# The expert loop of a hybrid block: TensorE, ScalarE and VectorE in an order set by hand

## Chip, cores and metric

One core of a Trainium2 chip runs the whole program. The metric is the device time of one execution in microseconds, the median of several runs.

## What is computed

The program is one layer of a hybrid model over 2048 tokens of width 1024: a token mixer with four branches, then a mixture of experts, then a norm. The change lies in the experts alone. A router gives each token two of 32 experts (`NE`), and

```python
def expert_block(args):
    xb, e = args
    return (jax.nn.silu(xb @ w1[e]) * (xb @ w3[e])) @ w2[e]
...
y_assign = out[dest].astype(jnp.float32) * weights[order][:, None]
return jax.ops.segment_sum(y_assign, tok_sorted, num_segments=n_tok).astype(h.dtype)
```

with `w1` and `w3` of 1024 x 512 and `w2` of 512 x 1024 in float32: 6.3 MB of weights for each expert, and 128 tokens on average.

## The kernel before

The functions of the experts stand inside `ffn`. The first 128 tokens of an expert are computed with float32 numbers split into a high part and the remainder: `split` (line 1224 casts on ScalarE, line 1225 subtracts on VectorE), and `mm3` (lines 1368 to 1370) makes three matmuls of each product. A panel is 128 x 1024 numbers, 0.52 MB. An expert has twelve: four of `w1`, four of `w3`, four of `w2`. `unit` (line 808) loads one into a buffer `mraw` and splits it into `mhi` and `mlo`. There are 16 raw buffers and 12 pairs of parts (`RAW, PARTS = 16, 12`), so a panel of the next expert takes the pair that the same panel of this expert leaves.

Tokens 129 to 192 of an expert are its small blocks, of 32 tokens each. They use the raw panels: `up_rest` and `down_rest` call `quarters` (line 930), which puts four column groups side by side, inside `tc.If` on the count of tokens (`guard`, loaded at line 1006 into a register of TensorE and of GpSimd). Their sums stand in two banks of PSUM of their own, `hu` and `hd` ("hf0" and "hf1"); two banks "tr" hold transposes, two "mm" the sums of `up`, two "sc" those of `down`.

The loop over the experts runs one expert ahead in parts. Its body, for expert e, is: the small up block (`up_rest`), its activation and gate (`gate_rest`), the first layer (`up`, with activation at line 903 and gate at 904), the transposes of the small result (`plain`, "hq"), the transposes of the next expert's gathered rows (`turn`, line 869 and 870, and `turn_rest`, line 877, with copies of the token weights at lines 884 and 892), the gather of the rows after those (`fetch`, on GpSimd), the panels of the next first layer, then the second layer of the expert before (`down`), this expert's `w2` panels, the small down block and the transposes of h (`parts`). Results are added to the rows in memory by indirect DMAs on GpSimd (line 908). `beyond` makes a table for tokens above 192 and is called in the fifth expert.

A transpose takes its bank, and the copy out of it follows at once in the program's text:

```python
def turned_into(put, src, r, n, w=128):
    for c in range(0, n, 512 // r):
        ...
        pt = psum("tr")
```

The text is not the order in which an engine runs: a scheduler lays out each engine's list before the run from its own estimates, and keeps only the dependencies. A `tc.If` stays a unit. On the chip each engine then works its list from the front.

Of the kernel before, what the change touches and what calls it, by code (L numbers as in the profile page):

```python
# [570 lines left out]
def ffn(tc, G, A, out, bcast, rsqrt, split, mm3, MT, MR, X1, FR, mid):  # L571
# [236 lines left out]
    def unit(src, q=nc.sync, eng=nc.vector):  # L808

        raw = rp.tile([128, 1024], F32, name="mraw")  # L810
        q.dma_start(raw, src)
        hi, lo = (wr.tile([128, 1024], F32R, name=n, bufs=PARTS) for n in ("mhi", "mlo"))
        split(raw, hi, lo, eng)
        return hi, lo, raw

# [39 lines left out]
    def turned_into(put, src, r, n, w=128):  # L855

        for c in range(0, n, 512 // r):
            m = min(n - c, 512 // r)
            pt = psum("tr")
            for k in range(m):  # L860
                nc.tensor.transpose(pt[:, k * r:(k + 1) * r], src[:, (c + k) * 128:(c + k + 1) * 128], G.ident[:r, :r])
            put(slice(c, c + m), pt[:, :m * r].rearrange("p (k t) -> p k t", t=r))

    def parts(src, n, name):

        hi, lo = (wp.tile([128, n, 128], F32R, name=name + c) for c in "hl")

        def put(c, v):
            nc.scalar.copy(hi[:, c], v)
            nc.vector.tensor_sub(lo[:, c], v, hi[:, c].bitcast(F32))  # L870
        turned_into(put, src, 128, n)
        return hi, lo

    def plain(src, n, name):

        t = wp.tile([128, n, 64], F32, name=name)
        turned_into(lambda c, v: nc.scalar.copy(t[:, c], v), src, 64, n)
        return t

    def turn(xg):  # L880

        p = parts(xg, 8, "x")
        w = wp.tile([128, 1], F32, name="w0", bufs=2)
        nc.scalar.copy(w, xg[:, D:D + 1])
        return p, w

    def turn_rest(xg):

        p = plain(xg, 8, "xq")
# [3 lines left out]
        return p, w  # L893

    def up(xw, w1, w3):

        x, w = xw
        pa = [psum("mm"), psum("mm")]
        for p, ws in zip(pa, (w1, w3)):
            mm3(p, lambda k: (x[0][:, k], x[1][:, k]),  # L900
                lambda k: tuple(t[:, (k % 2) * 512:(k % 2) * 512 + 512] for t in ws[k // 2][:2]), range(8))
        h = wp.tile([128, FF], F32, name="mh0")
        nc.scalar.activation(h, pa[0], AF.Silu)
        nc.vector.scalar_tensor_tensor(h, pa[1], w, h, op0=OP.mult, op1=OP.mult)
        return h
# [8 lines left out]
    def down(h, w2, dst, rest=()):  # L914

        y = wp.tile([128, D], F32, name="my0")
        py = [psum("sc"), psum("sc")]
        for c, (p, ws) in enumerate(zip(py, w2)):
            o = slice(512 * c, 512 * c + 512)
            mm3(p, lambda k: (h[0][:, k], h[1][:, k]), lambda k: tuple(t[:, o] for t in ws[k][:2]), range(4))  # L920
            nc.vector.tensor_mul(y[:, o], p, m5[:, o])  # L921
# [14 lines left out]
    def up_rest(xw, w1, w3, guard):  # L936

        w = [w1, w3]
        quarters(hu, 8, guard, lambda k, j: xw[0][:, k, j * 32:j * 32 + 32],
                 lambda k, g: w[g // 2][k // 2][2][:, (k % 2) * 512 + (g % 2) * 256:][:, 0:256])  # L940

    def gate_rest(xw):
        h = wp.tile([64, FF], F32, name="mh1")
        nc.scalar.activation(h, hu[0:64], AF.Silu)
        for j in range(2):
            o = slice(j * 256, j * 256 + 256)
            nc.vector.scalar_tensor_tensor(h[:, o], h[:, o], xw[1][:, j:j + 1], hu[64:128, o], op0=OP.mult, op1=OP.mult)
        return h

    def down_rest(h, w2, guard, e_):  # L950

        quarters(hd, 4, guard, lambda k, j: h[:, j * 2 + k % 2, (k // 2) * 32:(k // 2) * 32 + 32],
                 lambda k, g: w2[k][2][:, g * 256:g * 256 + 256])
# [12 lines left out]
    def in_weights(e_, q=nc.sync, eng=lambda n, u: nc.vector):  # L966
        f2 = lambda n, u: A[n][e_][:, 2 * u:2 * u + 2].rearrange("p k n -> p (k n)")
        return [[unit(f2(n, u), q, eng(n, u)) for u in range(4)] for n in ("e1", "e3")]
# [41 lines left out]
    x = turn(rows_[0]), turn_rest(rows_[1])  # L1010
# [4 lines left out]
    with tc.issue_after(listed.ins):  # L1015
        w13 = in_weights(0, eng=lambda n, u: nc.gpsimd if n == "e1" and u < 2 else nc.vector)
    last = None
    for e_ in range(NE + 1):
        if e_ < NE:
# [4 lines left out]
            up_rest(x[1], *w13, guard)  # L1024
            h1 = gate_rest(x[1])
            h = up(x[0], *w13)
            t1 = plain(h1, 4, "hq")
            q = nc.sync if e_ else nc.gpsimd
            if e_ + 1 < NE:
                x = turn(rows_[0]), turn_rest(rows_[1])  # L1030
# [21 lines left out]
    with tc.For_i(0, nov, 1) as it:  # L1052
# [23 lines left out]
        h = up(turn(gather(ix, 0, nullcontext)), w1, w3)  # L1076
        down(parts(h, 4, "h"), w2, ixs)
# [514 lines left out]
```

## Time and profile before

| | |
|---|---|
| median of 3 runs | 3157.36 us (3155.1 to 3159.68) |
| profiled execution | 3149.57 us, span 3147.7 us |
| TensorE busy | 2852.9 us, 91% |
| VectorE busy | 1827.1 us, 58% |
| ScalarE busy | 1160.4 us, 37% |
| the loop over the experts | 2238.7 to 3094.1 us of the span |

Busy time is the union of an engine's instructions; the ends of matmuls are modelled, so a row of matmuls that overlap counts as busy while the next one starts every 0.23 us. An engine's wait is the gap before an instruction, and what ended it is named behind the arrow. PEld is TensorE's weight loading; a "q" behind an engine's name is its sequencer, which evaluates branches and loads registers.

### The profile page before, as it was taken

The numbers are of one execution on the slowest core, as the hardware profiler recorded it, in microseconds if no ns is written. First come the engines' busy times: TensorE is split into PE (matmuls) and PEld (weight loads), VectorE is DVE, ScalarE is ACT, GpSimd is POOL, SyncE is SP. The second block draws the span as 40 slices with busy tenths as digits, with TensorE's granted clock in tenths as the row PEclk, the third lists the DMA queues.
The fourth block names the chain that finished last, engine by engine and source line by source line (L and its number), as shares of the span: only waits on it lengthen the run. The fifth ranks groups of instructions, "written<-read, shape, count | busy, mean of one in ns | idle before, by whom it ended". The sixth has DMA issues, their size and how long they took to land. (4 is left out here: it accounts for less than half of the span.)

```text
span 3147.7 us, 43618 instructions
## 1 busy us (share of the span) xinstructions
PE 2852.9 (91%) x15893; PEld 2229.4 (71%) x15893; DVE 1827.1 (58%) x2870; ACT 1160.4 (37%) x1722; POOL 583.6 (19%) x522
## 2 busy tenths in 40 slices
PE   7998999999867999899999999999588998999992
PEld 3887887777655677677777777888466676666662
DVE  4624125978776587433334334566678677777674
ACT  5411122322345032232223212322466566666552
POOL 3300010000014021013334333000211212112211
PEclk8999999999978899999999999999798999999996
DMA  7636244423128376765436434554788788888876
GB/s 295 243 111 210 87 158 154 144 81 110 52 72 277 124 225 202 254 237 194 134 120 207 131 125 149 187 169 148 268 292 276 262 300 279 303 289 286 273 235 238
DMA packets 245984, 621.48 MB, mean 197 GB/s; under 512 B 31128, under 2 KB 81464, under 8 KB 242008
## 3 DMA queue, kind: packets, MB, share of 16 engines
q1 hardware_dynamic: 211312, 506.17, 46.6%
q0 software_dynamic: 34416, 111.88, 12.4%
q8 instruction: 163, 2.67, 0.3%
q14 instruction: 93, 0.76, 0.1%
HBM read 484.86 MB, written 137.28 MB: 198 GB/s over the span
## 5 line engine op out<-in xcount | busy, mean ns | idle before, releaser
L1225 DVE TENSOR_TENSOR mlo<-mraw,mhi 128x1024 fp32r<-128x1024 f32 x382 | 447.8, 1225 | 61.4 <-ACT mhi L1224 61.3
L1224 ACT CAST mhi<-mraw 128x1024 fp32r<-128x1024 f32 x384 | 382.5, 1046 | 53.9 <-PE ps_mm L1370 16.1
L1368 PE MATMUL ps_mm<-hb1h,wlo 128*128 128x512 f32 x800 | 319.9, 400 | 2.6 <-DVE wlo L1225 2.6
L1369 PE MATMUL ps_mm<-hb1l,whi 128*128 128x512 f32 x800 | 317.9, 397 | 0.0
L1370 PE MATMUL ps_mm<-hb1h,whi 128*128 128x512 f32 x800 | 317.8, 397 | 0.0
L1519 ACT ACTIVATE ev<-ps_mm 128x512 f32<-128x512 f32 x128 | 76.3, 598 | 612.1 <-PE ps_mm L1370 511.5
L1225 DVE TENSOR_TENSOR wlo<-wraw,whi 128x1024 fp32r<-128x1024 f32 x164 | 214.9, 1319 | 145.1 <-ACT whi L1224 145.0
L1368 PE MATMUL ps_mm<-hb0h,wlo 128*128 128x512 f32 x672 | 270.0, 402 | 16.0 <-DVE wlo L1225 12.5
L1369 PE MATMUL ps_mm<-hb0l,whi 128*128 128x512 f32 x672 | 269.7, 401 | 0.0
L1370 PE MATMUL ps_mm<-hb0h,whi 128*128 128x512 f32 x672 | 267.9, 399 | 0.0
L1224 ACT CAST whi<-wraw 128x1024 fp32r<-128x1024 f32 x176 | 182.1, 1045 | 169.2 <-PE ps_mm L1370 69.8
L1569 POOL TENSOR_TENSOR macc<-macc,ev 128x512 f32<-128x512 f32 x96 | 165.8, 1727 | 309.0 <-DVE ev L1568 306.2
L1568 DVE TENSOR_TENSOR ev<-ev,ps_tr 128x512 f32<-128x512 f32 x96 | 65.8, 687 | 249.9 <-PE ps_tr L1370 243.4
L1369 PE MATMUL ps_mm<-mlo,xh 128*128 128x512 f32 x512 | 203.7, 398 | 6.9 <-PEq L928 3.0
L1368 PE MATMUL ps_mm<-mhi,xl 128*128 128x512 f32 x512 | 206.2, 403 | 1.8 <-ACT mhi L1224 1.4
L1370 PE MATMUL ps_mm<-mhi,xh 128*128 128x512 f32 x512 | 202.9, 396 | 2.5 <-PEq L928 2.2
L908 POOL DMA_INDIRECT d_X<-my,sct x51 | 100.7, 1974 | 444.6 <-DVE my L921 289.6
L1368 PEld LDWEIGHTS ps_mm<-hb1h,wlo 128*128 128x128 f32 x800 | 151.3, 189 | 37.0 <-issue 3.4
L1370 PEld LDWEIGHTS ps_mm<-hb1h,whi 128*128 128x128 f32 x800 | 151.2, 189 | 33.0 <-issue 2.4
L1369 PEld LDWEIGHTS ps_mm<-hb1l,whi 128*128 128x128 f32 x800 | 151.3, 189 | 32.2 <-issue 1.9
L1368 PEld LDWEIGHTS ps_mm<-hb0h,wlo 128*128 128x128 f32 x672 | 128.0, 191 | 45.9 <-DVE wlo L1225 14.3
L1369 PEld LDWEIGHTS ps_mm<-hb0l,whi 128*128 128x128 f32 x672 | 128.1, 191 | 29.3 <-issue 3.2
(588 smaller groups left out, 5898.7 us busy)
## 6 DMA issues: line engine op xcount, KB each, us to landing
mraw<-e SPq DMA_DIRECT2D x372, 512.0 KB
wraw<-wg SPq DMA_DIRECT2D x80, 512.0 KB
wraw<-wt SPq DMA_DIRECT2D x40, 512.0 KB
aw<-adaw SPq DMA_DIRECT2D x64, 256.0 KB
d_GS<-ev SPq DMA_DIRECT2D x64, 256.0 KB
ev<-d_GS POOLq DMA_DIRECT2D x64, 256.0 KB, 4.4
wraw<-wg POOLq DMA_DIRECT2D x24, 512.0 KB, 4.3
d_FR<-hb0h SPq DMA_DIRECT2D x22, 512.0 KB
```

The costliest lines, as they stand in the source:

```text
L908: d = nc.gpsimd.indirect_dma_start(out=out, out_offset=bass.IndirectOffsetOnAxis(ap=dst, axis=0), in_=y, in_offset=None, compute_op=OP.add)
L1224: nc.scalar.copy(hi, raw)
L1225: eng.tensor_sub(lo, raw, hi.bitcast(F32))
L1368: nc.tensor.matmul(ps, wl, xh, start=start and n == 0, stop=False)
L1369: nc.tensor.matmul(ps, wh, xl, start=False, stop=False)
L1370: nc.tensor.matmul(ps, wh, xh, start=False, stop=stop and n == len(ks) - 1)
L1519: nc.scalar.activation(g, ps, AF.Sigmoid)
L1568: nc.vector.tensor_mul(g, g, ps)
L1569: nc.gpsimd.tensor_add(acc, acc, g)
```

## The change

Each helper is cut into what TensorE does and what ScalarE and VectorE do with the result, so that the loop can place the halves apart. `in_order`, called between the pieces, chains all instructions of TensorE, ScalarE and VectorE traced since its last call, each behind the one before it on its engine (edges without a semaphore). SyncE and GpSimd stay with the scheduler.

```diff
+    def in_order():
+        traced = nc.cur_bb.bb.instructions
+        if queues.get("block") is not traced:
+            queues.clear()
+            queues.update(block=traced, at=len(traced))
+        for i in traced[queues["at"]:]:
+            if i.engine in (mybir.EngineType.PE, mybir.EngineType.Activation, mybir.EngineType.DVE):
+                if i.engine in queues:
+                    tc.add_manual_dep(i, queues[i.engine].name, mybir.DependencyInfo(
+                        mybir.DependencyClass.NoSync, mybir.DependencyReason.DATA), reason="in order")
+                queues[i.engine] = i
+        queues["at"] = len(traced)
...
-            pt = psum("tr")
+            pt = psum("tr") if bank is None else bank
...
     for e_ in range(NE + 1):
+        in_order()
+        more = e_ + 1 < NE
+        q = nc.sync if e_ else nc.gpsimd
+        if e_:
+            turned, h = parts(h, 4, "h")
+            turned()
+            in_order()
+            w2, w2n = [parted(t) for t in w2n], None
+            in_order()
         if e_ < NE:
             guard = guards[e_]
             if e_ + 2 < NE:
                 guards.append(over(load(e_ + 2)))
-            up_rest(x[1], *w13, guard)
-            h1 = gate_rest(x[1])
-            h = up(x[0], *w13)
-            t1 = plain(h1, 4, "hq")
-            q = nc.sync if e_ else nc.gpsimd
-            if e_ + 1 < NE:
-                x = turn(rows_[0]), turn_rest(rows_[1])
+            up_rest(x1, w13[:4], w13[4:], guard)
+            pa = up(x, w13[:4], w13[4:])
+            in_order()
+            raw = in_panels(e_ + 1, q) if more else []
+            w2n = [loaded(A["e2"][e_][:, u], q) for u in range(4)]
+            n13 = [parted(t) for t in raw[:4]]
+            hn, h1 = silu(pa), silu_rest()
+            in_order()
+            gate_rest(h1, w1)
+            out1, t1 = plain(h1, 4, "hq", hu)
+            n13 += [parted(t) for t in raw[4:7]]
+            out1()
+            if more:
+                out0, x = parts(rows_[0], 8, "x")
+                out1, x1 = plain(rows_[1], 8, "xq", hd)
+                out0()
+            in_order()
+            gate(pa, hn, w)
+            n13 += [parted(t) for t in raw[7:]]
+            if more:
+                out1()
+                w, w1 = weights(rows_[0]), weights_rest(rows_[1])
                 if e_ + 2 < NE:
                     rows_ = fetch(e_ + 2, lambda: guards[e_ + 2](0))
-                w13 = in_weights(e_ + 1, q)
-        if last:
-            down(last[0], [last[1]] * 2, sct[:, e_ - 1:e_], last[2])
+            in_order()
+        if e_:
+            placed(down(h, [w2] * 2), sct[:, e_ - 1:e_], rest)
+            in_order()
         if e_ < NE:
-            w2 = [unit(A["e2"][e_][:, u], q) for u in range(4)]
-            rest = down_rest(t1, w2, guard, e_)
-            last = parts(h, 4, "h"), w2, rest
-            if e_ == 4:
+            down_rest(t1, w2n, guard)
+            rest = placed_rest(guard, e_)
+            in_order()
+            h, w13 = hn, n13
+            if not more:
                 beyond()
```

`loaded` is the load of `unit`, `parted` its split; `silu`, `gate`, `silu_rest`, `placed` and `placed_rest` are the activations, gates and results that stood in `up`, `gate_rest`, `down` and `down_rest`; `weights` and `weights_rest` copy the token weights. `plain` gets a bank: `hu` for the small result, `hd` for the next rows. The rows that the engines' lists show for an expert late in the loop follow; `mh` is h, `xg` the gathered rows, `w` the token weights.

ScalarE, before, from the copy of the small result on (`w_23258` and `w_23245` are the weights of the expert after the one whose activation is `mh_23165`):

```order
L877 COPY hq<-ps_tr 128x256
L869 CAST xh<-ps_tr 128x512 x2
L849 UNCONDITIONAL_BRANCH
L877 COPY xq<-ps_tr 128x512
L892 COPY w_23258<-xg_16951 32x1 x2
L928 UNCONDITIONAL_BRANCH
L944 ACTIVATE mh_23165<-ps_hf_16946 64x512
L1224 CAST mhi<-mraw 128x1024 x2
L928 UNCONDITIONAL_BRANCH
L1224 CAST mhi<-mraw 128x1024 x2
L869 CAST hh<-ps_tr 128x512
L884 COPY w_23245<-xg_16950 128x1
```

and now, one expert:

```order
L891 CAST hh<-ps_tr 128x512
L956 UNCONDITIONAL_BRANCH
L1294 CAST mhi<-mraw 128x1024 x8
L923 ACTIVATE mh_22855<-ps_mm 128x512
L972 ACTIVATE mh_22857<-ps_hf_16946 64x512
L1294 CAST mhi<-mraw 128x1024 x3
L900 COPY hq<-ps_hf_16946 128x256
L891 CAST xh<-ps_tr 128x512 x2
L1294 CAST mhi<-mraw 128x1024
L900 COPY xq<-ps_hf_16947 128x512
L904 COPY w_22910<-xg_16950 128x1
L911 COPY w_22912<-xg_16951 32x1 x4
```

The weight copies stood in front of the small block's activation and between the casts; they are now the last of the expert.

TensorE, before, where a first layer ends and the second of the expert before begins:

```order
L1370 MATMUL ps_mm<-mhi,xh 128x512
L1368 MATMUL ps_sc<-mhi,hl 128x512
L861 MATMUL ps_tr<-c_kid,mh_22499 128x64 x2
L861 MATMUL ps_tr<-c_kid,xg_16950 128x128 x3
L861 MATMUL ps_tr<-c_kid,mh_22499 128x64 x2
L861 MATMUL ps_tr<-c_kid,xg_16950 128x128
L1369 MATMUL ps_sc<-mlo,hh 128x512
L1370 MATMUL ps_sc<-mhi,hh 128x512
L1368 MATMUL ps_sc<-mhi,hl 128x512
L861 MATMUL ps_tr<-c_kid,xg_16950 128x128 x4
```

and now:

```order
L1440 MATMUL ps_mm<-mhi,xh 128x512
L880 MATMUL ps_hf_16946<-c_kid,mh_22857 128x64 x4
L880 MATMUL ps_tr<-c_kid,xg_16950 128x128 x8
L880 MATMUL ps_hf_16947<-c_kid,xg_16951 128x64 x8
L868 COMPARE_AND_BRANCH
L868 UNCONDITIONAL_BRANCH x2
L1438 MATMUL ps_sc<-mhi,hl 128x512
```

The transposes of h1 ("mh") and of the rows shared the bank tag "tr" and stood between matmuls of the second layer; they now form one piece, with three kinds of bank.

VectorE, before, from the remainders of the next expert's panels on:

```order
L1225 TENSOR_TENSOR mlo<-mraw,mhi 128x1024 x5
L921 TENSOR_TENSOR my_23984<-ps_sc,m_16956 128x512 x2
L1225 TENSOR_TENSOR mlo<-mraw,mhi 128x1024 x4
L955 TENSOR_TENSOR my_24072<-ps_hf_16947,m5x 128x512
L870 TENSOR_TENSOR hl<-ps_tr,hh 128x512
L959 UNCONDITIONAL_BRANCH
L947 SCALAR_TENSOR_TENSOR mh_24164<-mh_24164,w_23924,ps_hf_16946 64x256 x2
L904 SCALAR_TENSOR_TENSOR mh_24218<-ps_mm,w_23911,mh_24218 128x512
L1225 TENSOR_TENSOR mlo<-mraw,mhi 128x1024
L870 TENSOR_TENSOR xl<-ps_tr,xh 128x512 x2
L1225 TENSOR_TENSOR mlo<-mraw,mhi 128x1024
L849 UNCONDITIONAL_BRANCH
```

and now:

```order
L949 TENSOR_TENSOR my_22619<-ps_sc,m_16956 128x512
L987 TENSOR_TENSOR my_22657<-ps_hf_16947,m5x 128x512
L991 UNCONDITIONAL_BRANCH
L956 UNCONDITIONAL_BRANCH
L892 TENSOR_TENSOR hl<-ps_tr,hh 128x512
L1295 TENSOR_TENSOR mlo<-mraw,mhi 128x1024 x8
L978 SCALAR_TENSOR_TENSOR mh_22857<-mh_22857,w_22581,ps_hf_16946 64x256 x2
L1295 TENSOR_TENSOR mlo<-mraw,mhi 128x1024 x3
L892 TENSOR_TENSOR xl<-ps_tr,xh 128x512 x2
L868 UNCONDITIONAL_BRANCH
L928 SCALAR_TENSOR_TENSOR mh_22855<-ps_mm,w_22579,mh_22855 128x512
L1295 TENSOR_TENSOR mlo<-mraw,mhi 128x1024
```

The gate of the small block (line 947, now 978) stood behind hl and is now between the eighth and the ninth remainder, the gate of the first layer (904, now 928) behind the rows' remainders.

## Rows read from the trace of the kernel before

**Rows 1.** The page, busy time of the engines over the span.

```profile
PE 2852.9 (91%) x15893; PEld 2229.4 (71%) x15893; DVE 1827.1 (58%) x2870; ACT 1160.4 (37%) x1722; POOL 583.6 (19%) x522
```

**Rows 2.** Windows: four stretches of whole experts, busy us (instructions) of each engine, clock, DMA.

```profile
core 0: us, PE busy (x) PEld busy (x) DVE busy (x) ACT busy (x) POOL busy (x), PEclk, DMA share, GB/s
2238.70:2285.70 47.00, 39.09 (x171) 28.89 (x169) 35.58 (x35) 32.00 (x48) 16.68 (x18) 0.90 0.84 311
2285.70:2403.20 117.50, 93.79 (x479) 68.85 (x476) 91.53 (x114) 70.08 (x102) 17.46 (x10) 0.89 0.78 261
2403.20:3065.90 662.70, 617.53 (x4102) 451.68 (x4101) 474.89 (x524) 405.39 (x601) 132.27 (x79) 0.95 0.84 283
3065.90:3094.10 28.20, 26.11 (x139) 19.54 (x136) 15.61 (x19) 7.69 (x10) 5.57 (x4) 1.00 0.28 43
```

**Rows 3.** Windows: three single experts, columns as in rows 2.

```profile
2636.20:2667.50 31.30, 26.24 (x163) 18.99 (x161) 18.93 (x22) 19.35 (x30) 2.65 (x2) 0.87 0.63 204
2745.60:2765.90 20.30, 20.00 (x99) 15.40 (x97) 15.51 (x18) 13.00 (x19) 6.77 (x4) 1.00 0.89 287
...
2901.70:2929.30 27.60, 27.14 (x227) 19.38 (x225) 19.04 (x22) 16.59 (x25) 7.31 (x4) 1.00 0.80 261
```

**Rows 4.** Waits over the loop: who waited for whom, us in total, times, longest.

```profile
ACT w L892 <- DMA xg<-d_FR,idx: 77.3, 15, 13.7
...
PE ps_tr L861 <- ACT hq L877: 20.6, 8, 4.0
...
PE ps_tr L861 <- DVE mh L947: 12.4, 2, 10.8
...
ACT mhi L1224 <- DMA mraw<-e: 3.3, 3, 2.7
```

**Rows 5.** Timeline of ScalarE: start, us, instruction, in brackets idle time before it.

```profile
2640.60 0.39 ACT L892 COPY w<-xg 32x1 f32<-32x1 f32 x2 [13.71 <-DMA xg<-d_FR,idx]
```

**Rows 6.** Timeline of TensorE: first matmul of a first layer, first one behind it.

```profile
2765.93 0.47 PE L1368 MATMUL ps_mm<-mhi,xl 128*128 128x512 f32 x1
...
2776.93 0.44 PE L1368 MATMUL ps_sc<-mhi,hl 128*128 128x512 f32 x1
```

**Rows 7.** Line 930, small matmuls: all up records; one up block; one down block.

```profile
L930 PE MATMUL ps_hf<-mraw,xq x1216: 379/379/636, 2316.5 to 3062.3; 128*32 128x256 f32 x174
...
2660.34 3.66 PE L930 MATMUL ps_hf<-mraw,xq 128*32 128x256 f32 x64
...
2896.95 1.93 PE L930 MATMUL ps_hf<-mraw,hq 128*32 128x256 f32 x32
```

**Rows 8.** VectorE: seven panel remainders in a row, and their group over the loop.

```profile
2887.40 8.02 DVE L1225 TENSOR_TENSOR mlo<-mraw,mhi 128x1024 fp32r<-128x1024 f32 x7
...
L1225 DVE TENSOR_TENSOR mlo<-mraw,mhi 128x1024 fp32r<-128x1024 f32 x382 | 447.8, 1225 | 61.4 <-ACT mhi L1224 61.3
```

**Rows 9.** Timeline of the last expert: transposes of h on TensorE, the copy on ScalarE.

```profile
3086.01 0.60 PE L861 MATMUL ps_tr<-c_kid,mh 128*128 128x128 f32 x4
...
3086.65 0.59 ACT L869 CAST hh<-ps_tr 128x512 fp32r<-128x512 f32 x1 [7.43 <-PE ps_tr L861]
```

**Rows 10.** Line 1006, loads of token counts on TensorE: ns min/median/max, first and last start.

```profile
L1006 PEldq TENSOR_LOAD <-cnti x32: 294/299/493, 2224.1 to 2382.9; - x32
L1006 PEldq FUSED_REGOPS  x32: 146/146/167, 2224.7 to 2383.3; - x32
```

**Rows 11.** DMA queues, 2403.2 to 3065.9 us: packets, MB, share of 16 engines.

```profile
q1 hardware_dynamic: 43342, 157.83, 64.9%
q0 software_dynamic: 10513, 28.58, 18.6%
```

**Rows 12.** VectorE groups of the table for surplus tokens: one wide, one half, one narrow.

```profile
L993 DVE TENSOR_TENSOR le<-le,ov 128x1024 bf16<-128x1024 bf16 x1 | 1.2, 1216 | 0.0
...
L982 DVE TENSOR_REDUCE ov<-le 128x32 f32<-128x480 bf16 x1 | 0.6, 640 | 0.0
...
L999 DVE TENSOR_SCALAR ej<-ej 128x32 f32<-128x32 f32 x1 | 0.2, 169 | 0.0
```

More of the change, by code (lines that the diff above doesn't have):

```diff
@@ L814, in unit @@
         return hi, lo, raw
+    queues = {}
+    def in_order():
[10 more added lines that the diff above has]
+        queues["at"] = len(traced)
     class InTurn:
@@ L866, in parts, with taken, plain, weights @@
         hi, lo = (wp.tile([128, n, 128], F32R, name=name + c) for c in "hl")
[L868 to L874, printed above, removed]
+        out = []
+        turned_into(lambda *a: out.append(a), src, 128, n)
+        def taken():
+            for c, v in out:
+                nc.scalar.copy(hi[:, c], v)
+                nc.vector.tensor_sub(lo[:, c], v, hi[:, c].bitcast(F32))
+        return taken, (hi, lo)
+    def plain(src, n, name, bank):
         t = wp.tile([128, n, 64], F32, name=name)
[L877 to L882, printed above, removed]
+        out = []
+        turned_into(lambda *a: out.append(a), src, 64, n, bank)
+        return lambda: [nc.scalar.copy(t[:, c], v) for c, v in out], t
+    def weights(xg):
         w = wp.tile([128, 1], F32, name="w0", bufs=2)
         nc.scalar.copy(w, xg[:, D:D + 1])
-        return p, w
-    def turn_rest(xg):
-        p = plain(xg, 8, "xq")
+        return w
+    def weights_rest(xg):
         w = wp.tile([64, 2], F32, name="w1", bufs=2)
@@ L912, in added, with down @@
         return d
-    def down(h, w2, dst, rest=()):
-        y = wp.tile([128, D], F32, name="my0")
+    def down(h, w2):
         py = [psum("sc"), psum("sc")]
@@ L920, in down, with placed @@
             mm3(p, lambda k: (h[0][:, k], h[1][:, k]), lambda k: tuple(t[:, o] for t in ws[k][:2]), range(4))
+        return py
+    def placed(py, dst, rest=()):
+        y = wp.tile([128, D], F32, name="my0")
+        for c, p in enumerate(py):
+            o = slice(512 * c, 512 * c + 512)
             nc.vector.tensor_mul(y[:, o], p, m5[:, o])
@@ L1015, in ffn @@
     with tc.issue_after(listed.ins):
-        w13 = in_weights(0, eng=lambda n, u: nc.gpsimd if n == "e1" and u < 2 else nc.vector)
-    last = None
+        w13 = [parted(t, nc.gpsimd if u < 2 else nc.vector) for u, t in enumerate(in_panels(0))]
+    w2n = w2 = None
     for e_ in range(NE + 1):
+        in_order()
[7 more added lines that the diff above has]
+            in_order()
         if e_ < NE:
@@ L1075, in ffn @@
         w2 = [InTurn(lambda u: dy("e2")[:, u], otiles) for _ in range(2)]
-        h = up(turn(gather(ix, 0, nullcontext)), w1, w3)
-        down(parts(h, 4, "h"), w2, ixs)
+        xg = gather(ix, 0, nullcontext)
+        out0, x = parts(xg, 8, "x")
+        out0()
+        w = weights(xg)
+        pa = up(x, w1, w3)
+        h = silu(pa)
+        gate(pa, h, w)
+        out0, h = parts(h, 4, "h")
+        out0()
+        placed(down(h, w2), ixs)
     for i, t in enumerate(x1s):
```

41 lines of the change are left out of this document (25 added, 16 removed).

## Prediction

> **What bounds the kernel now.** I first read the page for the engine that is full. TensorE is busy for 91% of the span [rows 1], so I looked for stretches where it is not, and the loop over the experts has most of them. I split it so that each stretch covers whole experts, from the first sum of one expert's first layer to that of a later one: two experts in 47.0 us, four in 117.5, twenty-five in 662.7, and the last one in 28.2, 855.4 us in all, or 26.7 per expert [rows 2]. TensorE's idle time there is 855.4 - 776.5 = 79 us, and the granted clock is 0.89 to 0.95 in the long stretches, so part of the busy time is also stretched. A mean of 26.7 hides two kinds of expert, so I looked at single ones [rows 3]. An expert with at most 128 tokens ("quiet") took 20.3 us with TensorE idle for 0.3. One with a small up block and two small down blocks took 27.6 with 0.5 idle. Those two are what TensorE's own work costs. Beside them stands an expert of 31.3 us with one small block, TensorE idle for 5.1 and a granted clock of 0.87.
>
> The waits name the cause [rows 4]. ScalarE waited 77.3 us in 15 places for gathered rows, in its copies of the token weights; TensorE waited 20.6 us before transposes for ScalarE's copy of hq, since those transposes and the next rows' share the two "tr" banks; and 10.8 us of its 12.4 for VectorE's gate of the small block are one stall, in the fifth expert. In the 31.3 us expert ScalarE stood 13.71 us before two such copies [rows 5]: in the old order they stand right behind the copy of the expert before, when the gather has barely been issued, and the small block's activation, the panel casts and the transposes' copies queue behind them. So what bounds this part is TensorE's work plus waits that the order makes.
>
> **The price of TensorE's work.** A first layer is 48 matmuls, 11.0 us from its first row to the first row behind it [rows 6]. The quiet 20.3 us hold this, 24 matmuls of the second layer, 24 transposes and three skipped branches. The up blocks are 1216 records, 64 per block: 19 blocks, in four places two in a row, so 15 experts have one; a run of 64 takes 3.7 us with its tail of 0.4, a down block's 32 take 1.9 [rows 7]. One more block of each kind, behind another, costs 3.3 + 1.5 = 4.8. Hence 27.6 - 1.5 = 26.1 us for an expert with one block of each.
>
> **The change, part by part.**
> The weight copies now stand behind the transposes of the same rows, which have waited for that gather already; ScalarE's waits of 77.3 us and what queues behind them go. The gather for the next expert is issued behind those copies, about 16 us before its transposes; I cost that at nothing, because TensorE's second layer and the next first layer (5.5 + 11.0 us) cover it. The small transposes now go to the banks "hf0" and "hf1", so the large transposes find both "tr" banks free, and the 20.6 us go.
>
> What is late next? The transposes of hq, right behind the first layer, wait for VectorE's gate of the small block, which has hl and eight panel remainders ahead of it. Seven remainders in a row took 8.02 us [rows 8], 1.13 each when one follows the other. From the start of the transposes of h it is 1.3 us to hl (3086.01 to the end of ScalarE's copy at 3087.24) [rows 9], then 0.7 + 8 x 1.13 + 0.9 for the two gates, about 12.1 with a hop. TensorE reaches that point after 0.4 of transposes, 0.7 for a count (below), 0.3 for a branch and 11.0 of matmuls, 12.4. That is nearly a tie; I take 0.3 us for quiet experts and none where a small block delays TensorE. Bounds: 0, and 3 us if each remainder follows its cast at 1.4 us, the pace at which the first layer frees four panels in half of 11.0.
>
> The loads of the token counts were drawn forward; on TensorE all 32 stand before 2383 [rows 10]. Chained, one stands in every expert behind the transposes of h. A load of 0.30 and 0.15 of register work are 0.45; with the gaps around them I charge 0.7 for each expert. [...]
>
> The splitting of w2 moves from the end of its expert to the start of the next; twelve casts and twelve remainders per expert stay. Busy time in the four stretches sums to 617.6 us on VectorE and 515.2 on ScalarE [rows 2], 19.3 and 16.1 per expert, both under 21.3, so they fit if nothing stalls them. The raw w2 panels are held longer, but the loads that follow need their buffers only some 10 us later.
>
> The queue of panel loads: the two queues were busy for 64.9 + 18.6% of 662.7 us [rows 11], 553 us, or 22.1 per expert. Quiet experts at 21.3 would be 0.8 us short; experts with blocks at 26.8 have 4.7 to spare, and four panels are read ahead. I take 0, with 14 x 0.8 = 11 as the other bound.
>
> The table for surplus tokens moves from the fifth expert to the last. Its four wide operations cost 1.2 us each, two of half the width half of that, some seventeen narrow ones up to 0.17 [rows 12], 8.9 us in all. Today they lie around the 10.8 us stall [rows 4]. In the new place VectorE runs them before hl of the last expert, and the four remainders of w2 stand behind: from the transposes of h 1.0 + 8.9 + 0.7 + 4.5, then 2.8 for the second half of the sums, is 38.2 after the last first layer began, against 28.2. That costs 10.
>
> **The sum.** Quiet: 20.3 + 0.7 + 0.3 = 21.3. With blocks: 26.1 + 0.7 = 26.8.
> Twenty-five experts: 11 x 21.3 + 14 x 26.8 + 4 x 4.8 for second blocks - 2.5 (the last down block lies behind) = 626, against 662.7: -36.
> Two at the start, where the panels are still coming at 311 GB/s: as before, 47.0. Four behind them: 3 x 21.3 + 26.8 = 90.7, against 117.5: -27.
> The last: +10. Nothing outside the loop moves. Together -53 us.
> The profiled execution took 3149.6 us, of which the span is 3147.7; the sum makes 3096 of it. The median of the runs shown is 3157.4, 7.8 above, so I forecast **3104 us**. A difference of 0.2% (6 us) is about what a measurement of this kernel can tell from none.
>
> **The rivals.**
> (a) *VectorE's chain sets the quiet experts.* If the remainders follow their casts at 1.4 us, the gate of the small block is 3 us late in 14 quiet experts instead of 0.3: +38, so -15 in all, 3142. For it: VectorE waited 61 us for casts today [rows 8]. Against it: a cast takes 1.05 us, less than a remainder, and of the eight panels ahead of the gate four have their buffers from the start.
> (b) *Slower: the panels of the second matrix come late.* They may be loaded only when the small up block has read the raw panels they replace, at the top of an expert; three of their casts stand ahead of the copies of hq and of the next rows. A panel takes 22.1 / 12 = 1.8 us of the shared queues, so the third lands 5.5 us after the first starts. Its cast stands behind hh (0.6), ten casts (1.05) and two activations (0.6 each), near 12. If loads still under way delay it by more than the 6 us between, ScalarE, then VectorE and TensorE wait. It turns the forecast's gain into a loss from 53 / 31 = 1.7 us of waiting per expert; at 3 us it is +93 - 53, 3197. [...] Against it: the queues are at 22.1 of a mean 25 us, and casts waited 3.3 us for panels in all [rows 4].
> (c) *More goes than I count.* With no wait for the gate, the count hidden behind the transposes, and 4 us less at the start, 14 x 1.0 + 15 x 0.7 + 4 = 28 more: -81, 3076.
> (d) *The waits only change place*, and the time stays at 3157.
>
> **How the numbers follow.** Forecast (-25 to -75) 0.62; (a) 0.13; (b) 0.10; (c) 0.10; (d) 0.05. Faster by over 0.2%: 0.62 + 0.13 + 0.10 = 0.85; the same 0.05; slower 0.10. The range runs from beyond (c), 3070, to 3150, short of (d); what lies outside is (b), (d) and a little of (c).
>
> **What would show it.** Right: ScalarE's waits for gathered rows under 15 us; TensorE's for hq gone; quiet experts at 20.5 to 22 us and those with blocks at 26 to 27.5; a granted clock of 0.98 or more from the third expert on; 9 us of idle TensorE in the last expert. Wrong: TensorE waiting before the transposes of hq for VectorE in most quiet experts (a), casts waiting for panels (b), or a mean expert above 26 us.

## The result, and the profile after

The change took 3116.56 us, median of 4 runs (3109.45 to 3122.46), beside 3156.23 for the kernel before (4 runs): a ratio of 0.9877, 95% interval 0.9848 to 0.9906. That is 39 us faster; 53 were forecast, 3104 us with a range of 3070 to 3150. The profiled executions differ by 34.2 us, 3149.57 against 3115.34. The first instructions of the loop stand where they stood (2239.8 us from the span's start, 2238.7 before), so all of it lies in the expert loop.

The page of the change, busy time of the engines; it answers to [rows 1]:

```profile
PE 2822.9 (91%) x15893; PEld 2229.4 (72%) x15893; DVE 1839.2 (59%) x2870; ACT 1154.0 (37%) x1722; POOL 574.3 (18%) x522
```

TensorE does the same 15893 matmuls in 30 us less busy time: most of the gain is clock (0.99 instead of 0.95 in the longest stretch). Windows of the change, the first three stretches of [rows 2] (us; busy us and instructions of TensorE, its weight loads, VectorE, ScalarE and GpSimd; granted clock, DMA share, GB/s):

```profile
2239.80:2289.70 49.90, 38.22 (x168) 29.78 (x169) 41.29 (x41) 34.51 (x51) 14.53 (x19) 0.83 0.87 324
2289.70:2385.80 96.10, 85.65 (x480) 66.55 (x481) 80.45 (x88) 67.47 (x101) 15.19 (x10) 0.97 0.93 309
2385.80:3023.30 637.50, 593.64 (x4096) 451.23 (x4096) 485.80 (x525) 399.58 (x601) 128.15 (x80) 0.99 0.88 294
```

Set against the forecast, stage by stage, in us of the profiled executions:

| stretch | before | forecast | after | forecast missed by |
|---|---|---|---|---|
| up to the loop | 2238.7 | 2238.7 | 2239.8 | +1.1 |
| first two experts | 47.0 | 47.0 | 49.9 | +2.9 |
| next four | 117.5 | 90.7 | 96.1 | +5.4 |
| next twenty-five | 662.7 | 626 | 637.5 | +11.5 |
| from the last expert's first sum to the end | 81.8 | 91.8 | 90.2 | -1.6 |

The misses add up to 19.3, which is 53 - 34 but for rounding. In the twenty-five experts the idle time of TensorE is nearly what it was, 637.50 - 593.64 = 43.9 us against 662.70 - 617.53 = 45.2 [rows 2]; busy time fell by 23.9, with the granted clock at 0.99 instead of 0.95. Busy time times clock is the same, 617.53 x 0.95 = 587 and 593.64 x 0.99 = 588. The long waits of [rows 4] are gone, the clock is higher, and short waits of the same sum came. Windows of three single experts of the change: a quiet one, one whose stretch holds an up block, one whose stretch holds the down block that belongs to it.

```profile
2597.10:2618.00 20.90, 19.60 (x96) 15.50 (x96) 18.85 (x21) 15.38 (x24) 7.72 (x5) 1.00 1.03 351
2618.00:2642.80 24.80, 23.29 (x160) 17.93 (x160) 22.40 (x25) 19.37 (x29) 3.33 (x3) 1.00 0.96 314
2642.80:2666.40 23.60, 21.51 (x128) 16.49 (x129) 16.55 (x19) 12.67 (x22) 4.29 (x3) 1.00 0.89 308
```

Quiet experts take 20.9 us. An up block adds 3.9, a down block 2.7. Waits from the loop's first sum to 3060 us (who waited for whom, us in total, times, longest):

```profile
PE ps_mm L1438 <- PEq L956: 24.2, 28, 4.4
...
PE ps_tr L880 <- DVE my L987: 11.9, 10, 1.2
...
PE ps_tr L880 <- PEq L956: 9.2, 16, 0.6
...
ACT mhi L1294 <- DMA mraw<-e: 8.9, 7, 2.9
...
PE ps_sc L1438 <- DVE hl L892: 8.6, 1, 8.6
...
PE ps_hf L880 <- ACT mhi L1294: 4.7, 1, 4.7
...
PE ps_tr L880 <- DVE mh L928: 4.7, 1, 4.7
...
PE ps_hf L880 <- DVE mh L978: 1.0, 5, 0.2
```

Of [rows 4] the first three are gone: no wait for hq, none of 10.8 us for a gate, and ScalarE has no wait for gathered rows in the loop. The last of them, the casts' wait for panels, grew from 3.3 us to 8.9. ([rows 4] counts only the copies of the small block's weights at line 892. Those at line 884 waited for gathered rows too in the kernel before, 21.6 us in six places, so it was 98.9 us in all.) What stands there now are the sequencer's branches (PEq L956 is the branch around a small block), the 8.6 us of the last expert, and, in the first expert alone, two waits of 4.7 us while panels still arrive. The wait "for VectorE's my" ahead of the transposes of h comes only behind a small down block that stands alone. One of them in TensorE's timeline (start, duration; in brackets the idle time before):

```profile
2661.79 1.93 PE L958 MATMUL ps_hf<-mraw,hq 128*32 128x256 f32 x32
2664.90 0.63 PE L880 MATMUL ps_tr<-c_kid,mh 128*128 128x128 f32 x4 [1.18 <-DVE my L987]
2666.41 0.47 PE L1438 MATMUL ps_mm<-mhi,xl 128*128 128x512 f32 x1 [0.87 <-PEq L956]
```

The down block ends at 2663.72, the transposes of h start 1.18 us later; in experts without a down block that gap is 0.57 (9.2 us in 16). Three branches around the scatter of the result (line 991) stand in it on TensorE's sequencer, 0.07, 0.21 and 0.17 us between 2664.18 and 2664.74; the quiet expert above has one there, 0.22 us at 2616.27. The trace has 66 records of that line's branch on TensorE's queue and 66 on GpSimd's: the program loads the count for both engines and tests it on both. The load of the next count, which the change puts behind these transposes, shows the same place (ns, shortest, median and longest of 32):

```profile
L1038 PEldq TENSOR_LOAD <-cnti x32: 297/318/1107, 2224.1 to 2970.8; - x32
```

It takes 0.30 us in experts without a down block, and 0.58 to 1.11 in the 13 that follow a down block.

### The profile page after: what moved, and what is told of

The parts are those of the page before. It is cut to its first block, busy times and chain, and to the rows that moved or that the text cites. A ratio compares the mean times of both kernels' runs of the same rounds, so it can differ in the third digit from the quotient of the medians.

```text
span 3113.5 us, 43212 instructions
## 1 busy us (share of the span) xinstructions
PE 2822.9 (91%) x15893; PEld 2229.4 (72%) x15893; DVE 1839.2 (59%) x2870; ACT 1154.0 (37%) x1722; POOL 574.3 (18%) x522
## 5 line engine op out<-in xcount | busy, mean ns | idle before, releaser
L1589 ACT ACTIVATE ev<-ps_mm 128x512 f32<-128x512 f32 x128 | 76.2, 597 | 618.5 <-PE ps_mm L1440 515.6
L1438 PE MATMUL ps_mm<-mhi,xl 128*128 128x512 f32 x512 | 205.7, 402 | 24.5 <-PEq L956 24.2
L869 POOL DMA_INDIRECT xg<-d_FR,idx x48 | 67.5, 1406 | 459.4 <-ACT w L904 444.1
```

Of the source, the lines that this page charges most:

```text
L869: nc.gpsimd.indirect_dma_start(out=xg, out_offset=None, in_=FR, in_offset=bass.IndirectOffsetOnAxis(ap=idx_ap, axis=0), bounds_check=2 * T ...
L1438: nc.tensor.matmul(ps, wl, xh, start=start and n == 0, stop=False)
L1589: nc.scalar.activation(g, ps, AF.Sigmoid)
```

## The experiments

**Theory T** at the start: the gain is ScalarE's wait for gathered rows, taken away, with the small transposes' bank as a second part; the order that the hand sets on TensorE costs something back. **Rivals**: the banks and the smaller pieces carry the gain, or the waits were covered by slack. Eleven variants and one repetition of the change ran; medians stand beside the kernel before on the same chip, in the same stretch of time. The loop's first sum stands anywhere from 2228 to 2250 us in their profiles, so traces are compared by stretches of the loop.

### 1. The change without its chain

```diff
     def in_order():
+        return
```

> The change without its chain: the pieces, their banks and their places in the text stay, but the scheduler orders the three engines again (its list for ScalarE puts the copies of the small block's weights between two casts, ahead of the next first layer, as before the change). Theory T (the gain is ScalarE's wait for gathered rows, taken away by the order): ScalarE waits 40 us or more for gathered rows again, and the time is 3140 to 3165 us. Rival R (the banks and the smaller pieces carry the gain, the order is not needed): within 0.3% of the change, 3107 to 3126 us.

Measured: 3189.4 us, ratio 1.0106 (1.0071 to 1.0141), 33 us slower than before. Waits of this run:

```profile
ACT w L912 <- DMA xg<-d_FR,idx: 114.0, 14, 14.1
...
PE ps_hf L959 <- ACT hq L901: 36.7, 7, 6.7
```

The scheduler draws the weight copies forward again, and ScalarE stands 114 us before those of the small block alone, more than before [rows 4]; TensorE waits again for hq, now with its own bank. Theory T's waits are there, and the time is worse than T gave: the pieces and banks alone lose. The order is what makes the change pay.

### 2. One thing put back: the early weight copies

```diff
+                w, w1 = wn
                 if e_ + 2 < NE:
                     rows_ = fetch(e_ + 2, lambda: guards[e_ + 2](0))
+                    wn = weights(rows_[0]), weights_rest(rows_[1])
-                w, w1 = weights(rows_[0]), weights_rest(rows_[1])
```

> The change with one thing put back: the copies of the token weights of the rows after next stand right behind the issue of their gather, at the end of ScalarE's work for an expert, so ScalarE waits there for each gather. A gather lands 7.2 us after its issue (5.3 to 8.1), and ScalarE has some 4.8 us idle there in a quiet expert. Theory T: everything behind on ScalarE is 2 to 4 us late, TensorE waits in most experts, and the time is 3150 to 3200 us. Rival R (the wait for the gather was covered by slack on ScalarE): 3117 to 3127 us, although the wait is seen.

Measured: 3166.65 us, ratio 1.0021 (0.9997 to 1.0044): the whole gain is gone. Waits of this run:

```profile
ACT w L904 <- DMA xg<-d_FR,idx: 180.0, 32, 8.5
...
PE ps_hf L880 <- DVE mh L978: 12.6, 6, 4.6
```

ScalarE waits once per expert, 180 us in all, and what stands behind is late: the gate of the small block, for which TensorE waits 12.6 us (1.0 in the change), and the cast hh, for which it waits 9.2 (4.2). In the first of these rows and in [rows 5] ScalarE stood idle until the copy's rows had landed, up to 8.5 us here and 13.71 there, and no cast passed the copy that waited. The time lies in theory T's range, and the rival falls. TensorE's waits are fewer than T had, though: six for the gate, not one in most experts. And the run is no exact return to the order before: it makes ScalarE wait 180 us where the kernel before had 98.9, and it has the longer gaps behind down blocks of runs 6 and 7 (14.8 us in nine places, 1.7 at most).

### 3. The kernel before, with the weight copies alone put behind their rows

```diff
+    def behind():
+        a, b = [i for i in nc.cur_bb.bb.instructions if i.engine == mybir.EngineType.Activation][-2:]
+        tc.add_manual_dep(b, a.name, ...)
...
         nc.scalar.copy(w, xg[:, D:D + 1])
+        behind()
...
             nc.scalar.copy(w[h * 32:h * 32 + 32, j:j + 1], xg[j * 32:j * 32 + 32, D:D + 1])
+            behind()
```

> The kernel before, with one thing of the change alone: each copy of token weights is chained on ScalarE behind the copy of the same rows that stands before it in the text; all else is left to the scheduler. Theory T: ScalarE's waits for gathered rows fall from 77 to under 15 us, TensorE's for hq fall too since hq's copy queued behind them, and the time falls by 20 to 35 us, to 3121 to 3136. Rival R (what counts is the shared transpose banks or the moved table): it falls by less than 8 us.

Measured: 3107.54 us, ratio 0.9839 (0.9808 to 0.9869): 48 us faster than before, more than was expected, and no less than the whole change. Its twenty-five experts by the windows, and a wait in the loop:

```profile
2399.90:3024.20 624.30, 601.45 (x4102) 441.37 (x4101) 474.15 (x524) 412.68 (x605) 149.33 (x79) 0.99 0.89 301
```

```profile
PE ps_tr L861 <- DVE mh L954: 15.0, 3, 12.3
```

Against 662.7 us at a clock of 0.95 [rows 2], 624.3 at 0.99, and here the idle time fell too, to 22.9 us. No wait of ScalarE for gathered rows is left, and TensorE's waits for hq went with them (0.2 us is left), although the banks are still shared. One long wait stands: the transposes of the small result waited 12.3 us for the gate of the small block, which VectorE ran behind the table for surplus tokens.

### 4. As 3, with the banks

```diff
+            pt = psum("tr") if bank is None else bank
...
+        p = plain(xg, 8, "xq", hd)
...
+            t1 = plain(h1, 4, "hq", hu)
```

> As the run before it (weight copies behind their rows' copies in the kernel before), and the small transposes by way of the banks of the small blocks' sums. Theory T: the hq waits of TensorE (20.6 us before) that the first edit leaves go, some 5 to 10 us more than that run: 3113 to 3130. Rival R (the bank was the cause, the weight copies not): this run alone has the gain, and the run before it has none.

Measured: 3081.38 us, ratio 0.9757 (0.9727 to 0.9787): 75 us faster than before, 26 beyond run 3 where 5 to 10 were expected, and its interval lies clear of the change's. The windows of the four experts ahead of the twenty-five, in run 3 and in this run; those of this run's twenty-five; and a wait in the loop:

```profile
2292.70:2399.90 107.20, 88.84 (x478) 66.25 (x476) 91.05 (x113) 68.37 (x98) 17.74 (x10) 0.93 0.81 276
```

```profile
2290.80:2380.10 89.30, 84.58 (x479) 64.57 (x477) 78.20 (x96) 64.10 (x96) 20.76 (x9) 1.00 0.95 333
2380.10:2998.60 618.50, 593.78 (x4104) 441.46 (x4102) 488.20 (x543) 411.68 (x608) 190.55 (x79) 0.99 0.91 306
```

```profile
PE ps_hf L861 <- DVE my L962: 6.0, 2, 5.5
```

The 618.5 us hold the stall of the table for surplus tokens, which in this kernel still belongs to the fifth expert: TensorE waited 5.5 us for VectorE there. Theory T's reason fails: the waits for hq were gone in run 3 already, so the 26 us can't be they. By the traces the loop is 28 us shorter: 18 in the four experts, where the 12.3 us wait of run 3 is gone and the clock is at 1.00, 4 in the first two, and 6 in the twenty-five. What each is due to beyond that one wait was not tried apart.

### 5. The banks alone, in the kernel before

The bank edits of 4 without `behind`.

> The kernel before, with the small transposes by way of the banks of the small blocks' sums alone, all else as before (with the weight copies chained as well it took 3081 us, with those alone 3108, against 3156 before). Theory T (both waits are separate): ScalarE's waits for gathered rows stay above 60 us, TensorE's for hq (20.6 us) go, the time falls by 10 to 26 us. Rival R (the late copies decide, the bank helps only once they are gone): it falls by less than 6 us, and other transposes or the small blocks wait for the late copy instead.

Measured: 3156.75 us, ratio 0.9994 (0.9978 to 1.0009): nothing. Waits of this run:

```profile
ACT w L892 <- DMA xg<-d_FR,idx: 73.1, 12, 13.5
ACT w L884 <- DMA xg<-d_FR,idx: 53.1, 17, 6.4
...
PE ps_hf L861 <- DVE my L955: 21.6, 5, 5.7
...
PE ps_hf L930 <- ACT hq L877: 21.2, 9, 3.6
```

ScalarE waits 126 us for gathered rows, against 98.9 before on the same two lines, and TensorE's 20.6 us before the transposes [rows 4] have become 21.2 before the small down blocks, for the same copy of hq, and 21.6 before transposes into the new bank, for a result that VectorE has not read yet. The rival was right: hq's copy is late because ScalarE stands, and another bank does not bring it sooner. By the trace the nothing is a sum: the first six experts take 148.4 us instead of 164.5, with the 10.8 us wait of [rows 4] gone, and the twenty-five take 679.1 instead of 662.7. With ScalarE's waits gone, the same edit is worth 26 us (4 against 3). So the two parts don't add: 48 + 0 against 75.

### 6. The count load moved behind the first layer

```diff
             pa = up(x, w13[:4], w13[4:])
+            if e_ + 2 < NE:
+                guards.append(over(load(e_ + 2)))
```

(It stood ahead of the small up block.)

> The change, with TensorE's load of the token count of the expert after next moved from behind the transposes of h to behind the matmuls of the first layer (TensorE's sequencer and GpSimd's issue the same number of loads). Theory T (the prediction's term: a load in the chain costs TensorE up to 0.7 us per expert where it stands between short transposes and a branch): behind 48 matmuls most of it is hidden, 30 x 0.3 to 0.6 us, so 9 to 18 us faster than the change, 3099 to 3108 us. Rival R (the gap there is the branch, not the load): within 4 us of the change.

Measured: 3110.39 us, ratio 0.9859 (0.9837 to 0.9881), which can't be told from the change. The loads (ns) and TensorE's waits:

```profile
L1038 PEldq TENSOR_LOAD <-cnti x32: 297/304/490, 2223.0 to 2968.4; - x32
```

```profile
PE ps_tr L880 <- DVE my L987: 16.5, 10, 1.7
...
PE ps_mm L1438 <- PEq L956: 11.0, 15, 2.2
```

Loads are at 0.30 us in the median and 0.49 at most, and the wait for the branch ahead of the first layer fell from 24.2 to 11.0 us. The wait ahead of the transposes of h, behind down blocks, stayed, and was longer in this run, 16.5 us in as many places as 11.9 (see 7). So the load is slow only where the change puts it, 0.58 us and more behind down blocks, and the transposes' wait is not the load's. The time lies between the two expectations and decides nothing.

### 7. The table spread over the experts

```diff
     def beyond():
         nc.vector.tensor_scalar(thr, i32_[:, :J], 128.0, float(FIT), op0=OP.mult, op1=OP.add)
+        yield
...
+        if e_ > 3:
+            next(table, None)
         if e_:
             placed(down(h, [w2] * 2), sct[:, e_ - 1:e_], rest)
...
-            if not more:
-                beyond()
```

> The change, with the table for surplus tokens not computed in one piece in the last expert, but one of its 22 operations per expert from the fifth expert on, on VectorE just ahead of the results of the second layer, its table in a buffer of its own. Theory T (the last expert pays for the table: TensorE waited 8.57 us there for hl): that wait goes and nothing else is late, 7 to 9 us faster than the change, 3107 to 3110 us. Rival R (VectorE has no slack in the experts, 18.9 of 20.9 us busy in quiet ones): the gain is given back, less than 3 us.

Measured: 3128.73 us, ratio 0.9907 (0.9882 to 0.9931): no gain in all. In its trace the 8.6 us wait is gone, but behind down blocks TensorE waited longer than in the change. Its timeline there, and the load:

```profile
2806.59 0.63 PE L880 MATMUL ps_tr<-c_kid,mh 128*128 128x128 f32 x4 [1.62 <-DVE my L987]
2809.05 0.76 PE L1453 MATMUL ps_mm<-mhi,xl 128*128 128x512 f32 x1 [1.83 <-PEq L956]
2809.61 0.63 PE L1454 MATMUL ps_mm<-mlo,xh 128*128 128x512 f32 x1
2810.04 0.63 PE L1455 MATMUL ps_mm<-mhi,xh 128*128 128x512 f32 x1
```

```profile
L1052 PEldq TENSOR_LOAD <-cnti x32: 298/314/1554, 2230.5 to 3001.1; - x32
```

1.62 us before the transposes and 1.83 before the first layer, against 1.18 and 0.87 above, and then matmuls every 0.43 us where 0.23 is usual. Neither wait is for VectorE's table. Runs 2, 6 and 7, three different programs on one chip, all show some 1.6 us there, and the change 1.2 both times it was profiled, the second time (run 9) on another chip than theirs. Whether the length belongs to the chip or to where the code lies was not settled. So run 7 shows that the last expert's wait goes, and not what spreading the table is worth; run 11 tells more.

### 8. Registers of their own

```diff
-    load = lambda e_: nc.values_load(cnti[0:1, e_:e_ + 1], engines=ENGINES, min_val=0, max_val=CAP)
+    load = lambda e_, on: nc.values_load(cnti[0:1, e_:e_ + 1], engines=[on], min_val=0, max_val=CAP)
...
-            rest = placed_rest(guard, e_)
+            rest = placed_rest(guards_pool[e_], e_)
```

> The change, with the token counts loaded by TensorE and GpSimd into registers of their own instead of one for both, so that the branches around GpSimd's gathers and scatters are no longer evaluated on TensorE too (it evaluates those around its own small blocks alone). Theory T (branches between short pieces cost TensorE time: in the trace of the change the three around the scatter took 0.07, 0.21 and 0.17 us ahead of the transposes of h): 0.3 to 0.7 us per expert, 9 to 22 us faster than the change, 3095 to 3108 us. Rival R (these branches are hidden behind the drain of TensorE's own matmuls): within 4 us of the change.

Measured: 3106.62 us, ratio 0.9842 (0.9815 to 0.987), 10 us under the change, with overlapping intervals. TensorE behind the down block that ends at 2660.29, the loads, and the windows of its twenty-five experts:

```profile
2661.27 0.63 PE L880 MATMUL ps_tr<-c_kid,mh 128*128 128x128 f32 x4 [0.97 <-PEq L956]
```

```profile
L1038 PEldq TENSOR_LOAD <-cnti x32: 296/304/493, 2227.6 to 2958.4; - x32
```

```profile
2388.20:3012.30 624.10, 589.90 (x4097) 448.73 (x4097) 490.53 (x530) 404.19 (x605) 130.46 (x81) 0.99 0.91 301
```

The gap is 0.97 us on the chip on which runs 6 and 7 had 1.6, and the load, which stands where the change has it, is at 0.30 in the median and 0.49 at most. The twenty-five experts of this run take 624.1 us (637.5 in the change). Theory T holds by the trace, not by the time alone: with registers of their own TensorE's waits before the transposes of h are 1.0 us at most (15.7 us in 27 places; 1.2 in the change), and the load behind them is short. That is not all of the 13.4 us, for two stalls of the change, 4.43 and 2.39 us (see 9), are not in this run, where the longest wait for a branch ahead of a first layer is 2.7.

### 9. The change once more

> The change itself once more, beside the three runs below, so that each of them is held against the change on one chip (the trace of the change and those of its variants differ in how long TensorE's load of a count takes behind a small down block: 0.6 to 1.1 us in the one, 1.3 to 1.6 us in two variants). If that belongs to the chip, this run shows 1.3 to 1.6 us, and its time lies above 3117 us; if it belongs to the code of a variant, 0.6 to 1.1 us and 3107 to 3126 us.

Measured: 3119.75 us, ratio 0.9895 (0.9869 to 0.9921), beside 3152.65 for the kernel before. The loads and the twenty-five experts:

```profile
L1038 PEldq TENSOR_LOAD <-cnti x32: 297/313/1523, 2211.9 to 2958.7; - x32
```

```profile
2373.00:3011.30 638.30, 595.30 (x4096) 452.94 (x4096) 485.86 (x526) 399.67 (x601) 128.81 (x79) 0.99 0.89 293
```

The stretch is 638.3 us (637.5 in the first profile); the longest load took 1.52 us, which lies in the range given for the chip, the waits before the transposes of h behind down blocks are those of the change (12.0 us in ten places, 1.3 at most, against 11.9 and 1.2), and the time fits both: the question stays open. Two long stalls of TensorE, 4.43 and 2.39 us in the first profile of the change, are back at the same lines, 4.4 and 2.4 us, so they belong to the program and not to chance. This is the yardstick of the three runs that follow, on the same chip.

### 10. The chain on ScalarE alone

```diff
-            if i.engine in (mybir.EngineType.PE, mybir.EngineType.Activation, mybir.EngineType.DVE):
+            if i.engine == mybir.EngineType.Activation:
```

> The change with the chain on ScalarE alone; TensorE and VectorE are left to the scheduler, which puts branches and transposes between the matmuls of the first layer. Theory T (ScalarE's order makes the gain, and the hand's order on TensorE, with transposes, branches and a count load one behind the other, costs it 0.8 us or more per expert): 3080 to 3100 us, quiet experts at 20.0 to 20.5 us. Rival R (TensorE's order by hand costs nothing): 3107 to 3126. Rival S (it is needed: the scheduler's order on TensorE lets the engines wait for one another again): above 3130.

Measured: 3088.93 us, ratio 0.9789 (0.9761 to 0.9817): 31 us under the change beside it. Twenty-five experts and one quiet expert by the windows:

```profile
2387.60:3002.50 614.90, 589.63 (x4096) 441.21 (x4096) 479.17 (x529) 389.69 (x600) 140.22 (x80) 1.00 0.91 305
2684.70:2705.10 20.40, 19.79 (x97) 15.41 (x97) 17.25 (x19) 15.58 (x24) 0.59 (x2) 1.00 0.99 338
```

614.9 us against 638.3, quiet experts at 20.4. With TensorE left to the scheduler the count loads are drawn forward (the last at 2410 us), and the branches around the scatter stand between matmuls of the first layer instead of between a down block and the transposes. ScalarE still never waits for gathered rows in the loop. Theory T holds in the main: ScalarE's order makes the gain, and the hand's order on TensorE and VectorE together gives part of it back. Which of these two does was not tried apart.

### 11 and 12. The best of both

Run 11 is the change with the edits of 6, 7 and 8; run 12 the kernel of run 4 with those of 7 and 8.

> The change with the count load behind the first layer, registers of their own for TensorE and GpSimd, and the table for surplus tokens one operation per expert. If the three add (about 6, 10 and 8 us): 3088 to 3100 us, the last expert without the 8.57 us wait, count loads at 0.30 us throughout. If they share one cost: 3100 to 3110.

> The kernel before with the weight copies chained behind their rows' copies and the small transposes by way of the small blocks' banks (3081 us), and also registers of their own for TensorE and GpSimd and the table one operation per expert. In the run without these two the table cost 5.5 us of TensorE's time in one expert. If both help: 3065 to 3076 us; if the scheduler spoils the order around the new pieces: above 3081.

Measured: run 11 3092.74 us, ratio 0.9817 (0.9791 to 0.9844), 27 under the change beside it; run 12 3072.96 us, ratio 0.9747 (0.9719 to 0.9776), 80 under the kernel before and 47 under the change. The windows of their twenty-five experts, run 11 first:

```profile
2391.40:3006.20 614.80, 586.00 (x4097) 440.51 (x4097) 497.04 (x551) 403.96 (x605) 130.15 (x81) 1.00 0.92 306
```

```profile
2379.70:2983.30 603.60, 587.91 (x4066) 436.98 (x4065) 482.51 (x529) 397.70 (x604) 162.86 (x79) 1.00 0.92 314
```

In run 11 the three edits add as expected: 614.8 us in the experts, and from the last expert on, which is the span less the window's end, 3090.9 - 3006.2 = 84.7 us instead of 3101.3 - 3011.3 = 90.0. With run 9 beside it on one chip, that answers run 7: 5.3 us of the 8.6 stay gained. Run 11 keeps the hand's order on all three engines and can't be told from run 10, 614.8 us against 614.9 in the experts: the order on TensorE and VectorE is not shown to cost anything beyond the shared branches, the load and the table that it laid bare, and these can be moved within it. Run 12 beats both kernels; against run 4 its gain is within the intervals.

## Why the prediction was right, point by point

**The diagnosis** held. "ScalarE waited 77.3 us for gathered rows, and what queues behind": taking that alone away gives 48 us (run 3), and a wait for each gather at the end of ScalarE's work takes the whole gain (run 2). The 77.3 left out the 21.6 us of line 884, which the change takes away as well.

**The banks**: "the 20.6 us go" was right for the change, and the reading behind it, a cost of its own, was not. Alone the edit gives nothing (run 5), since the copy was late for another reason, and the weight copies alone leave 0.2 us of that wait (run 3). So that term was right in the sum by luck. What the banks do give on top of the weight copies, 26 us, lies mostly in the four experts that hold the table's stall (run 4).

**Quiet experts** were put at 21.3 and took 20.9. They were charged 1.0 above the floor of before, 0.3 for a gate and 0.7 for the load, and cost 0.6; TensorE waited for the gate of the small block 1.0 us in five places, 0.2 at most, so rival (a) falls. Rival (b) falls as well: casts waited 8.9 us for panels instead of 3.3, but behind the first expert the profile names a cast of panels for one wait of TensorE alone, the 2.39 us below, and the casts of that layer's panels had ended 9 us before the wait did.

**Experts with blocks** were put 5.5 us above quiet ones; they are 3.9 + 2.7 = 6.6 above. This is the term that was mis-sized. I took a down block's price from a row of before where it stood among matmuls; in the change it stands at a seam, with the scatter's branches behind it, and the gap grows from 0.57 to 1.18 us and the load from 0.30 to 0.58 or more. Put into the sum: 11 x 20.9 + 14 x 27.5 + 4 x 4.8 - 2.5 = 632. Most of the other 6 of 637.5 lies in two experts: 3.7 in one whose first layer waited 2.39 us at its second matmul, and 1.7 in the one behind a branch for which TensorE waited 4.43 (the longest of the first line of the waits above). That branch itself is most of the 5.4 by which the next four experts missed. Both come again at the same lines in run 9, 4.4 and 2.4 us, and what makes them long there is open. The sum has no term for such stalls, although branches of up to 7.05 us stood in the trace of the kernel before:

```profile
L928 PEldq COMPARE_BRANCH  x124: 65/179/7047, 2246.0 to 3081.7; - x124
```

The two waits of the change, and the window of TensorE's matmuls behind the first (columns as above):

```profile
2385.82 0.76 PE L1438 MATMUL ps_mm<-mhi,xl 128*128 128x512 f32 x1 [4.43 <-PEq L956]
2386.38 0.63 PE L1439 MATMUL ps_mm<-mlo,xh 128*128 128x512 f32 x1
2386.81 0.63 PE L1440 MATMUL ps_mm<-mhi,xh 128*128 128x512 f32 x1
...
2809.93 0.59 PE L1439 MATMUL ps_mm<-mlo,xh 128*128 128x512 f32 x1 [2.39 <-ACT mhi L1294]
```

```profile
2385.80:2389.70 3.90, 3.88 (x10) 3.09 (x11) 2.00 (x2) 1.08 (x2) 0.00 (x0) 0.52 0.86 246
```

Matmuls 0.43 us apart, and 0.23 from 2389.68 on: the granted clock was 0.52 in these 3.9 us and 1.00 from 2389.7 to 2393.0. By these rows that stall cost 1.8 us beyond its own length (9 matmuls x 0.2).

**The first two experts** were put at 47.0 and took 49.9: in the first one the fixed order makes TensorE wait 4.7 us each for a cast and for a gate while panels arrive, where the free order had 6.0 us idle in all. Rival (c) counted on the opposite.

**The last expert**: +10 forecast, +8.4 measured. VectorE, first operation of the table and the one behind it:

```profile
3043.34 0.16 DVE L1009 TENSOR_SCALAR thr<-i__14714 128x15 f32<-128x15 f32 x1
...
3052.04 0.68 DVE L892 TENSOR_TENSOR hl<-ps_tr,hh 128x512 fp32r<-128x512 f32 x1
```

8.70 us from the one to the other, ahead of hl, for which TensorE waited 8.6.

**The clock** came to 0.97 in the four experts and 0.99 in the twenty-five; at least 0.98 was forecast.

So the forecast held in sign and range, and for the reason given in its main part. The gain was 14 us smaller, 19 by the profiles. About 6 of these are the block term, because the seams of a hand-set order on TensorE were priced from rows where the scheduler had hidden them (14 x 0.7 = 10, of which quiet experts gave back 11 x 0.4 = 4); about 9 are the two stalls and the slow clock behind them (0.52 for 3.9 us, and 0.51 from 2809.9 to 2812.85); most of the rest is the first two experts. That the order on TensorE and VectorE was not needed (run 10), and that two small edits to the old kernel give nearly twice the gain (run 4), the prediction had not seen.

## What to carry to other kernels

When an engine stands before an instruction that waits for a transfer, and work queues behind it (77.3 us on ScalarE here [rows 4]), move the waiting instruction behind one that needs the same transfer anyway, before touching buffers: a second bank was worth nothing while the queue stood (3156.75 us, run 5), and 26 us once it ran (runs 3 and 4), most of them in four experts where the shared banks had let one other stall through to TensorE. Chain first only the engine whose order is wrong: here the scheduler spread branches and loads between long rows of matmuls and hid them, and the hand-set order laid them bare until they were moved (614.9 and 614.8 us in the twenty-five experts of runs 10 and 11, 638.3 in run 9). Price an instruction by rows with the neighbours it will have, not by those it has.

## What the runs showed of the hardware that was not expected

A load of one register on TensorE took 0.30 us nearly everywhere (0.299 in the median before, 0.318 in the change), but 0.58 to 1.11 in the change right behind a small down block, where the scatter's branches stand on TensorE's queue too (the longest was 1.55 in run 7 and 1.52 in run 9), and 0.49 at most with registers of their own (run 8). A branch on TensorE's sequencer took 0.18 us in the median, and 4.17 once in the loop of the change, where it made the wait of 4.43; the clock was 0.52 in the 3.9 us behind it, and run 9 has a wait of 4.4 us at the same line. The kernel before has six of 3.7 to 7.0 us in the loop, partly covered by matmuls. In run 7, behind waits of 1.62 and 1.83 us around one group of transposes, the next expert, a quiet one, took 23.5 us at a clock of 0.88, where the same expert of the change, behind waits of 1.17 and 0.90 us, took 20.8 at 1.00.
